# A four-layer diffusion trunk on one core: boundary operations moved into PSUM, and the first loads rearranged

## The chip, the cores and the metric

The kernel runs on one core of one Trainium2 chip. The metric is the device time of one execution in microseconds, lower being better; a kernel's time is the median of its runs. Only that time counts: neither the host nor the loading of the program is in it.

## What is computed

256 context tokens and 256 latent tokens of width 1024 go through four layers, and the latent ones come out. A layer is a token mixer and a SwiGLU feed-forward block (FFN, hidden width 2816). The mixers are differential attention (layers 0 and 3), windowed grouped-query attention (layer 1) and a bidirectional Mamba-2 scan (layer 2). In layer 3 only the latent tokens are carried past the mixer's keys and values. Each block sits in the same frame, where the six modulation vectors m of a layer come from a small product of the conditioning vector with `ada_w` (adaLN):

```python
m_lat = (act_lat @ ada_w[i] + ada_b[i]).reshape(b, N_MOD, 1, D)
u_lat = modulate(rmsnorm(h_lat, norm_g[i, 0]), m_lat[:, 0], m_lat[:, 1])   # t * (1 + scale) + shift
o_ctx, o_lat = mixer(u_ctx, u_lat, ...)
h_lat = h_lat + m_lat[:, 2] * rmsnorm(o_lat, norm_g[i, 1])
u_lat = modulate(rmsnorm(h_lat, norm_g[i, 2]), m_lat[:, 3], m_lat[:, 4])
h_lat = h_lat + m_lat[:, 5] * rmsnorm(swiglu(u_lat, ffn_w_in[i], ffn_w_out[i]), norm_g[i, 3])
```

The context tokens go through the same lines with `m_ctx`.

## The kernel before

**Products.** Everything is float32 made of two parts. A weight block of 128 x 1024 (512 KB) is loaded by a DMA that SP issues, ACT casts it to the high part `wh` (L261), and POOL, or for some blocks DVE, subtracts to get the low part `wl` (L263). Activations are split in the same way into `uh` and `ul`. A product is then three matmuls per 128 rows of weight: wh with uh, wh with ul, wl with uh (L285 to L287, L295 to L297).

**Tokens.** There are four tiles of 128 tokens: t0 and t1 are the context, t2 and t3 the latent ones. The residual stream `h` (`hall`) lies in SBUF, 128 tokens x 1024 a tile.

**A boundary** is what lies between the last product of a block and the first of the next, and it is done tile by tile. `project` (L495) multiplies out two halves of 512 columns into PSUM buffers "mm". Where partial sums exist it adds them into the SBUF tile `om` (L511). `gated` (L425) takes ACT's sum of squares of a half (L429), and DVE multiplies the half by the gate row into `om` (L430). `residual` (L432) adds the two sums (L436), makes a reciprocal root out of nine small 128x1 operations on DVE (`rsqrt`, L376 to L384) and adds the scaled 128x1024 tile to `h` in one instruction (L439). `normed` (L441) squares the new `h` on ACT (L447), makes a second root (L448, L376 to L384), scales the halves (ACT L456, DVE L454) into `sq`, and TensorE transposes them into PSUM "sm" (L460). `modulate` (L464) applies scale and shift, alternately on ACT (L475) and DVE (L473), into the SBUF tile `tm`, then casts `uh` (L477) and subtracts for `ul` (L478). The next block's matmuls read these.

**The FFN** (`unit` in L551) multiplies a gate into "mm" and an up part into "sc"; ACT takes Silu (L560), DVE multiplies into the SBUF tile `hd` (L561), ACT casts it (L563) and DVE subtracts (L564). There are 100 such units.

**adaLN.** The modulation weights come in blocks of 512 KB through a ring of four buffers "wa" (L308), 16 blocks for a pair of vectors. `ada_mm` multiplies four column groups into PSUM "ad" (L319); after the sixteenth ACT copies it out (L325), TensorE transposes it (L334), and `ada_finish` adds the bias (L341), adds 1 to a scale (L345) and multiplies by the norm's gain (L346).

**The start** (`run`, L1353): the context tiles are normed and copied to `oall` (L1370), the first 16 adaLN blocks run through the ring, three weight blocks are loaded, the latent half of `h` is loaded once the third is there (L1376, L1377), and the context tiles are modulated. The layer-0 mixer needs SBUF that `h` occupies, so `h_spill` (L703) writes it to DRAM (L708) and `h_reload` brings it back.

**Order.** A scheduler places the instructions of each engine once, when the program is built; each engine's queue is then worked off strictly in order. PSUM has eight buffers of 512 columns: three "mm", two "sc", two "sm", one "ad".

Of the kernel before, what the change touches and what calls it, by code (L numbers as in the profile page):

```python
# [177 lines left out]
class Trunk:  # L178
# [246 lines left out]
    def gated(self, src, t, x, row, ss):  # L425

        nc = self.nc
        q = self.t([P, 512], "tm", 2)
        nc.scalar.activation(q, src, AF.Square, scale=1.0 / 32, accum_out=ss[:, x : x + 1])  # L429
        nc.vector.tensor_tensor(out=self.om[t][:, 512 * x : 512 * x + 512], in0=src, in1=row, op=AL.mult)  # L430

    def residual(self, t, ss):  # L432

        nc = self.nc
        y, m = (self.t([P, 1], f"rs_{x}1", 4) for x in ("y", "m"))
        nc.vector.tensor_scalar(out=m, in0=ss[:, 0:1], scalar1=ss[:, 1:2], scalar2=EPS, op0=AL.add, op1=AL.add)  # L436
        self.rsqrt(y, m, 1)
        h = self.hall[:, t, :]
# [999 lines left out]
```

## Time and profile before

| | us |
|---|---|
| median of 3 runs | 2905.99 (2902.37 to 2906.01) |
| profiled execution | 2899.41 |
| its span | 2897.6, 37494 instructions |
| mean granted TensorE clock | 0.961 |

The profile is of one execution, and its times are microseconds from the start of the span. A busy share is a mean over the whole span. A timeline row says when an instruction started and how long it took, and in brackets how long its engine had been idle before it and what it waited for. The rows of a window give the busy time of each engine in one stretch; the stretch less TensorE's busy time (PE) is its idle time there.

### The profile page before, as it was taken

What the parts mean: (1) busy time and instruction counts of PE and PEld (TensorE: products, weight loads), DVE (VectorE), ACT (ScalarE), POOL (GpSimd) and SP (SyncE); (2) the same over time, 40 slices, a digit from 0 to 9 for tenths busy, and PEclk for the clock granted to TensorE, in tenths of its full rate; (3) what the DMA queues carried; (4) which work ended last, traced back from release to release, by engine and by line L of the source; (5) the groups of instructions that cost most, each with busy time, mean ns of one, the idle gap of its engine ahead of it and who ended that gap; (6) DMA issues with size and microseconds to landing.
All of it is one profiled execution on the core that took longest, in us unless ns stands there. A gap on an engine that the chain in (4) does not pass through costs nothing. (4 is left out here: it accounts for less than half of the span.)

```text
span 2897.6 us, 37494 instructions
## 1 busy us (share of the span) xinstructions
PE 2620.8 (90%) x14134; PEld 2110.0 (73%) x14134; DVE 1574.4 (54%) x2955; ACT 1236.4 (43%) x2439; POOL 1098.3 (38%) x525
## 2 busy tenths in 40 slices
PE   6999989999889989999888888879899998897898
PEld 3777677777776787777686666667777776786797
DVE  4676652222577662222588898866522226667444
ACT  4555443222357643222345555554432224554543
POOL 2322044334321053333333444433343343334585
PEclk8999999999999999999998999999999999999899
DMA  7433335544221145544231111132344442323352
GB/s 290 138 109 121 131 128 184 173 173 150 88 94 45 44 138 175 175 174 149 82 97 37 59 44 62 63 105 96 121 176 175 174 145 86 101 86 126 124 182 88
DMA packets 108325, 355.40 MB, mean 123 GB/s; under 512 B 14064, under 2 KB 24688, under 8 KB 105840
## 3 DMA queue, kind: packets, MB, share of 16 engines
q1 hardware_dynamic: 107568, 351.66, 36.0%
q8 instruction: 111, 1.82, 0.3%
q10 hardware_dynamic: 576, 1.34, 0.1%
q14 instruction: 70, 0.57, 0.1%
HBM read 329.36 MB, written 13.63 MB: 118 GB/s over the span
## 5 line engine op out<-in xcount | busy, mean ns | idle before, releaser
L263 POOL TENSOR_TENSOR wl<-wr,wh 128x1024 fp32r<-128x1024 f32 x356 | 863.5, 2432 | 1499.3 <-ACT wh L261 1360.0
L261 ACT ACTIVATE wh<-wr 128x1024 fp32r<-128x1024 f32 x356 | 376.0, 1057 | 809.4 <-PE mm L286 291.8
L285 PE MATMUL mm<-uh,wh 128*128 128x512 f32 (+1 forms) x1496 | 529.9, 355 | 16.3 <-ACT uh L477 15.0
L286 PE MATMUL mm<-ul,wh 128*128 128x512 f32 (+1 forms) x1496 | 526.9, 352 | 0.1
L287 PE MATMUL mm<-uh,wl 128*128 128x512 f32 (+1 forms) x1496 | 526.7, 352 | 0.0
L561 DVE TENSOR_TENSOR hd<-sc,sg 128x512 f32<-128x512 f32 (+1 forms) x100 | 56.9, 568 | 603.6 <-PE sc L287 599.0
L285 PEld LDWEIGHTS mm<-uh,wh 128*128 128x128 f32 x1496 | 289.3, 194 | 73.7 <-ACT uh L477 15.9
L287 PEld LDWEIGHTS mm<-uh,wl 128*128 128x128 f32 x1496 | 289.4, 193 | 34.4 <-issue 3.6
L286 PEld LDWEIGHTS mm<-ul,wh 128*128 128x128 f32 x1496 | 289.8, 194 | 32.5 <-issue 1.5
L285 PE MATMUL sc<-uh,wh 128*128 128x512 f32 (+1 forms) x800 | 273.7, 342 | 0.0
L287 PE MATMUL sc<-uh,wl 128*128 128x512 f32 (+1 forms) x800 | 273.7, 342 | 0.0
L286 PE MATMUL sc<-ul,wh 128*128 128x512 f32 (+1 forms) x800 | 273.6, 342 | 0.0
L296 PE MATMUL mm<-wh,hid 128*128 128x512 f32 x616 | 244.6, 397 | 0.0
L297 PE MATMUL mm<-wl,hid 128*128 128x512 f32 x616 | 244.0, 396 | 0.0
L295 PE MATMUL mm<-wh,hid 128*128 128x512 f32 x616 | 243.6, 396 | 0.0
L564 DVE TENSOR_TENSOR hid<-hd,hid 128x512 fp32r<-128x512 f32 (+1 forms) x100 | 207.5, 2075 | 65.8 <-ACT hid L563 65.8
L285 PEld LDWEIGHTS sc<-uh,wh 128*128 128x128 f32 x800 | 153.1, 191 | 17.6 <-issue 0.8
L286 PEld LDWEIGHTS sc<-ul,wh 128*128 128x128 f32 x800 | 153.2, 191 | 16.9
L287 PEld LDWEIGHTS sc<-uh,wl 128*128 128x128 f32 x800 | 153.2, 192 | 16.8
L595 DVE TENSOR_TENSOR o<-mm,o 128x512 f32<-128x512 f32 x84 | 58.0, 691 | 157.8 <-PE mm L297 157.8
L295 PEld LDWEIGHTS mm<-wh,hid 128*128 128x128 f32 x616 | 115.7, 188 | 35.9 <-ACT hid L563 4.2
L263 POOL TENSOR_TENSOR wl<-wa,wh 128x1024 fp32r<-128x1024 f32 x49 | 118.9, 2426 | 59.2 <-ACT wh L261 58.8
(300 smaller groups left out, 4851.5 us busy)
## 6 DMA issues: line engine op xcount, KB each, us to landing
wa<-in_adaw SPq DMA_DIRECT2D x192, 512.0 KB, 5.2
wr<-in_fin SPq DMA_DIRECT2D x154, 512.0 KB, 3.5
wr<-in_fout SPq DMA_DIRECT2D x77, 512.0 KB, 3.5
wr<-in_ssi SPq DMA_DIRECT2D x40, 512.0 KB, 3.5
wr<-in_daqk SPq DMA_DIRECT2D x24, 512.0 KB, 3.8
wa<-in_fin SPq DMA_DIRECT2D x22, 512.0 KB, 3.6
hspill<-h SPq DMA_DIRECT2D x8, 1024.0 KB, 4.0
h<-hspill SPq DMA_DIRECT2D x8, 1024.0 KB, 6.3
```

Source lines behind the costliest of these rows:

```text
L261: nc.scalar.activation(h, raw, AF.Copy)
L263: eng.tensor_tensor(out=l, in0=raw, in1=f32(h), op=AL.subtract)
L285: mm(out, wh, ah[ka][:, a:b], start=j == 0, stop=False)
L286: mm(out, wh, al[ka][:, a:b], start=False, stop=False)
L287: mm(out, wl, ah[ka][:, a:b], start=False, stop=j == len(todo) - 1)
L295: mm(out, ah[ka][:, tk], wt.h[:, kw, :], start=j == 0, stop=False)
L296: mm(out, al[ka][:, tk], wt.h[:, kw, :], start=False, stop=False)
L297: mm(out, ah[ka][:, tk], wt.l[:, kw, :], start=False, stop=j == len(todo) - 1)
L561: nc.vector.tensor_tensor(out=hd[:, :w], in0=pu[:, :w], in1=sg[:, :w], op=AL.mult)
L564: nc.vector.tensor_tensor(out=hl[:, a:b], in0=hd[:, :w], in1=f32(hh[:, a:b]), op=AL.subtract)
L595: nc.vector.tensor_tensor(out=o, in0=ps, in1=o, op=AL.add)
```

## The change

The two halves of a projection stay in the PSUM buffer that they were multiplied into: half 0 in "mm", half 1 in "sc". The partial sum is added and the gate row multiplied in place. The residual is two instructions of 512 columns, half 0 to `h`, half 1 to its PSUM buffer, which the squares and the scaling read directly; ACT copies it to `h` after the transposes (`settle`). The reciprocal root has six 128x1 operations instead of nine, all of the form tensor times per-partition scalar, with the squares scaled by G to fit. `modulate` works in place in PSUM, the FFN unit multiplies in place in its "sc" buffer, and `ada_finish` works in PSUM with the 1 added to the bias once at setup. At the start the first 12 adaLN blocks get buffers of their own (pool "first"), the other 4 the ring's; the context norm stays in PSUM ("sm" for t0, "sc" for t1); the latent half of `h` is loaded behind the first two weight blocks. The first `h_spill` writes nothing, since `h` is still the input `h0`.

```diff
@@ ada_load, ada_finish
-        raw = self.t([P, 2, 512], "wa", self.ADA_T)
+        raw = self.t([P, 2, 512], "wa", self.ADA_T) if pool is None else self.t([P, 2, 512], "w0", 12, pool=pool)
...
-            tt(out=mv, in0=pj[:, :, :, 0:2], in1=bias.unsqueeze(3).to_broadcast([P, 2, 4, 2]), op=AL.add)
+            tt(out=mv if n is None else pj, in0=pj, in1=bias.to_broadcast([P, 2, 4, 2]), op=AL.add)
             if n is not None:
-                if j in (1, 4):
-                    nc.vector.tensor_scalar(out=m, in0=m, scalar1=1.0, scalar2=None, op0=AL.add)
-                tt(out=m, in0=m, in1=self.ng[:, i, n, :].unsqueeze(2).to_broadcast([P, KD, 2]), op=AL.mult)
+                gain = self.ng[:, i, n, :].rearrange("p (q f) -> p q f", q=2).unsqueeze(3).to_broadcast([P, 2, 4, 2])
+                tt(out=mv, in0=pj, in1=gain, op=AL.mult)
@@ new: rsqrt1, squares, root, settle
+        ts(out=b.bitcast(I32), in0=m.bitcast(I32), scalar1=-0.5, scalar2=1597463007.0 - 2.0**31, op0=AL.mult, op1=AL.add)
+        ts(out=a, in0=b, scalar1=b, scalar2=m, op0=AL.mult, op1=AL.mult)
+        ts(out=a, in0=a, scalar1=-10.0 / 3, scalar2=a, op0=AL.add, op1=AL.mult)
+        ts(out=b, in0=a, scalar1=5.0, scalar2=b, op0=AL.add, op1=AL.mult)
+        ts(out=a, in0=b, scalar1=b, scalar2=m, op0=AL.mult, op1=AL.mult)
+        ts(out=y, in0=a, scalar1=-64.0 / 3, scalar2=b, op0=AL.add, op1=AL.mult)
...
+        self.nc.scalar.activation(q, src, AF.Square, scale=G / 32, accum_out=ss)
...
+        self.nc.scalar.activation(self.hall[:, t, 512:], hp, AF.Copy)
@@ residual
-        nc.vector.scalar_tensor_tensor(out=h, in0=self.om[t], scalar=y, in1=h, op0=AL.mult, op1=AL.add)
+        for x in range(2):
+            h = self.hall[:, t, 512 * x : 512 * x + 512]
+            self.nc.vector.scalar_tensor_tensor(
+                out=pss[1] if x else h, in0=pss[x], scalar=y, in1=h, op0=AL.mult, op1=AL.add
+            )
@@ normed, modulate
-        nc.scalar.activation(n, h, AF.Square, scale=1.0 / 32, accum_out=ss)
+        for x in range(2):
+            self.squares(hs[x], ss[:, x : x + 1])
...
+        if hp is not None:
+            self.settle(t, hp)
...
-                nc.vector.tensor_scalar(out=tm[:, k], in0=src[:, k], scalar1=a, scalar2=b, op0=AL.mult, op1=AL.add)
+                nc.vector.tensor_scalar(out=src[:, k], in0=src[:, k], scalar1=a, scalar2=b, op0=AL.mult, op1=AL.add)
...
-        nc.vector.tensor_tensor(out=ul, in0=tm, in1=f32(uh), op=AL.subtract)
+        nc.vector.tensor_tensor(out=ul, in0=src, in1=f32(uh), op=AL.subtract)
@@ project
-                ps = self.psum("mm")
+                ps = pss[t, x] = self.psum("sc" if x else "mm")
...
-                    nc.vector.tensor_tensor(out=src, in0=ps, in1=src, op=AL.add)
-                self.gated(src, t, x, rows[s, x], ss[t])
+                    nc.vector.tensor_tensor(out=ps, in0=ps, in1=o, op=AL.add)
+                self.squares(ps, ss[t][:, x : x + 1])
+                nc.vector.tensor_tensor(out=ps, in0=ps, in1=rows[s, x], op=AL.mult)
@@ ffn unit
-                nc.vector.tensor_tensor(out=hd[:, :w], in0=pu[:, :w], in1=sg[:, :w], op=AL.mult)
+                nc.vector.tensor_tensor(out=pu[:, :w], in0=pu[:, :w], in1=sg[:, :w], op=AL.mult)
...
-            nc.vector.tensor_tensor(out=hl[:, a:b], in0=hd[:, :w], in1=f32(hh[:, a:b]), op=AL.subtract)
+            nc.vector.tensor_tensor(out=hl[:, a:b], in0=pu[:, :w], in1=f32(hh[:, a:b]), op=AL.subtract)
@@ h_spill
+            self.hs = self.ins["h0"]
+            return self.t([P, KD * NT], "h")
@@ run
-                early[t, g] = self.oall[:, 4 * g : 4 * g + 4, t * P : (t + 1) * P]
-                self.nc.scalar.activation(early[t, g], ps, AF.Copy)
-        self.ada_flush(first, 1)
...
+            for t in range(16):
+                self.ada_load(*self.adaq.pop(0), None if t >= 12 else pool)
+            for n in range(2):
+                self.load_w(n)
+            self.nc.sync.dma_start(out=self.hall[:, 2:4], in_=self.ins["h0"][:, 2:4])
+            for t in TILES["c"]:
+                for g, ps in enumerate(self.normed(t, tag=("sm", "sc")[t])):
+                    early[t, g] = ps
+            while self.adaw:
+                self.ada_mm()
+            self.ada_finish("mm")
```

In the lists of instructions that follow, a name ends in the number of its buffer, and `out<-in` stands with the shape that is written.

The boundary of layer 3 between mixer and FFN, DVE, tile t2, before: gate multiply (L430), first root (L436 to L384) and residual (L439).

```order
L430 TENSOR_TENSOR o_84<-mm_22008,dq_21900 128x512
L436 TENSOR_SCALAR rs_m_4008_22037<-ss_21950 128x1
L376 TENSOR_SCALAR rs_y_4007_22036<-rs_m_4008_22037 128x1
L377 TENSOR_SCALAR rs_h_4009_22039<-rs_m_4008_22037 128x1
L378 TENSOR_TENSOR rs_a_4010_22040<-rs_y_4007_22036 128x1
L379 TENSOR_TENSOR rs_a_4010_22040<-rs_a_4010_22040,rs_m_4008_22037 128x1
L380 SCALAR_TENSOR_TENSOR rs_a_4010_22040<-rs_a_4010_22040 128x1
L381 SCALAR_TENSOR_TENSOR rs_y_4007_22036<-rs_a_4010_22040,rs_y_4007_22036 128x1
L382 TENSOR_TENSOR rs_a_4010_22040<-rs_y_4007_22036 128x1
L383 TENSOR_TENSOR rs_a_4010_22040<-rs_a_4010_22040,rs_h_4009_22039 128x1
L384 SCALAR_TENSOR_TENSOR rs_y_4007_22036<-rs_a_4010_22040,rs_y_4007_22036 128x1
L439 SCALAR_TENSOR_TENSOR h_21885<-o_84,rs_y_4007_22036,h_21885 128x1024
```

The same piece with the change:

```order
L532 TENSOR_TENSOR sc_21841<-sc_21841,dq_21733 128x512
L442 TENSOR_SCALAR rs_m_3929_21869<-ss_21783 128x1
L387 TENSOR_SCALAR rs_b_3931_21872<-rs_m_3929_21869 128x1
L388 TENSOR_SCALAR rs_a_3932_21873<-rs_b_3931_21872,rs_m_3929_21869 128x1
L389 TENSOR_SCALAR rs_a_3932_21873<-rs_a_3932_21873 128x1
L390 TENSOR_SCALAR rs_b_3931_21872<-rs_a_3932_21873,rs_b_3931_21872 128x1
L391 TENSOR_SCALAR rs_a_3932_21873<-rs_b_3931_21872,rs_m_3929_21869 128x1
L392 TENSOR_SCALAR rs_y_3930_21871<-rs_a_3932_21873,rs_b_3931_21872 128x1
L452 SCALAR_TENSOR_TENSOR h_21718<-mm_21785,rs_y_3930_21871,h_21718 128x512
L452 SCALAR_TENSOR_TENSOR sc_21841<-sc_21841,rs_y_3930_21871,h_21718 128x512
L442 TENSOR_SCALAR rs_m_3936_21887<-rs_s_3933_21882 128x1
```

The gate multiply and the residual now name PSUM buffers (`mm`, `sc`) where `o` stood, the root is seven instructions instead of ten, and every 128x1 one is a TENSOR_SCALAR.

The boundary between layer 0's FFN and layer 1's mixer, PE, the transposes of t2 (L460) among the mixer's first context matmuls, before:

```order
L285 MATMUL mm_6800<-uh_82,wh_6226 128x256
L286 MATMUL mm_6800<-ul_83,wh_6226 128x256
L287 MATMUL mm_6800<-uh_82,wl_6227 128x256
L285 MATMUL mm_6800<-uh_82,wh_6226 128x256
L460 MATMUL sm_6558<-cst_base_67,sq_6543 128x128 x4
L460 MATMUL sm_6564<-cst_base_67,sq_6543 128x128 x4
L286 MATMUL mm_6800<-ul_83,wh_6226 128x256
L287 MATMUL mm_6800<-uh_82,wl_6227 128x256
```

The same with the change (the transposes are L479):

```order
L284 MATMUL mm_6706<-uh_84,wh_6168 128x256
L285 MATMUL mm_6706<-ul_85,wh_6168 128x256
L286 MATMUL mm_6706<-uh_84,wl_6169 128x256
L284 MATMUL mm_6706<-uh_84,wh_6168 128x256
L479 MATMUL sm_6498<-cst_base_67,sq_6496 128x128 x4
L479 MATMUL sm_6504<-cst_base_67,sq_6496 128x128 x4
L285 MATMUL mm_6706<-ul_85,wh_6168 128x256
L286 MATMUL mm_6706<-uh_84,wl_6169 128x256
```

Before, 40 matmuls of the mixer stand between the FFN's last matmul and these transposes; with the change 10 do.

The start, SP, from the last two of the first 16 adaLN loads on, before:

```order
L308 DMA wa_198<-in_adaw 128x1024
L308 DMA wa_202<-in_adaw 128x1024
L260 DMA wr_229<-in_daqk 128x1024
L260 DMA wr_235<-in_daqk 128x1024
L260 DMA wr_271<-in_daqk 128x1024
L1344 DMA cst_att_378<-in_cst_att 128x640
L260 DMA wr_277<-in_dav 128x1024
L1377 DMA h_72<-in_h 128x2048
L260 DMA wr_283<-in_dav 128x1024
L770 DMA sublnr_391<-in_subln 128x1
L708 DMA hspill<-h_72 128x2048 x2
```

With the change, from the thirteenth of them on:

```order
L307 DMA wa_114<-in_adaw 128x1024
L307 DMA wa_116<-in_adaw 128x1024
L307 DMA wa_118<-in_adaw 128x1024
L307 DMA wa_120<-in_adaw 128x1024
L259 DMA wr_122<-in_daqk 128x1024
L259 DMA wr_128<-in_daqk 128x1024
L1399 DMA h_72<-in_h 128x2048
L259 DMA wr_261<-in_daqk 128x1024
L259 DMA wr_267<-in_daqk 128x1024
L259 DMA wr_273<-in_dav 128x1024
L1370 DMA cst_att_370<-in_cst_att 128x640
```

The load of the late half of `h` (`h_72<-in_h`) stands behind five weight blocks before (one of them ahead of this piece) and behind two with the change, and the two `hspill` writes are gone.

## Rows read from the trace of the kernel before

**Rows 1.** The page, part 1: busy time of each engine.

```profile
PE 2620.8 (90%) x14134; PEld 2110.0 (73%) x14134; DVE 1574.4 (54%) x2955; ACT 1236.4 (43%) x2439; POOL 1098.3 (38%) x525
```

**Rows 2.** Windows, seven boundaries: stretch, length, busy by engine, PEclk, DMA share, GB/s.

```profile
372.00:388.00 16.00, 8.27 (x46) 5.84 (x45) 12.05 (x19) 6.31 (x9) 9.63 (x5) 0.81 0.83 292
767.00:812.00 45.00, 31.23 (x179) 27.37 (x178) 36.40 (x79) 23.37 (x43) 22.39 (x12) 0.85 0.40 132
1012.00:1042.00 30.00, 21.63 (x124) 17.89 (x122) 22.78 (x38) 17.31 (x32) 20.31 (x8) 0.89 0.60 210
1415.00:1456.00 41.00, 28.48 (x157) 25.00 (x156) 31.70 (x68) 20.02 (x37) 19.31 (x12) 0.83 0.40 129
2004.00:2048.00 44.00, 30.80 (x167) 25.71 (x167) 33.59 (x75) 21.50 (x36) 20.11 (x8) 0.81 0.43 144
2424.00:2476.00 52.00, 34.55 (x191) 30.70 (x190) 38.07 (x84) 25.37 (x47) 22.93 (x12) 0.80 0.40 128
2663.00:2702.00 39.00, 16.58 (x80) 13.63 (x80) 25.95 (x60) 18.34 (x33) 11.76 (x5) 0.69 0.22 67
```

**Rows 3.** Windows, four short stretches (columns as in rows 2).

```profile
0.00:5.00 5.00, 0.00 (x0) 0.00 (x0) 0.27 (x1) 1.50 (x2) 2.29 (x8) 1.00 0.63 203
10.00:15.00 5.00, 5.00 (x22) 1.75 (x18) 2.39 (x15) 2.21 (x4) 0.00 (x0) 1.00 1.03 411
392.00:395.00 3.00, 3.00 (x28) 3.00 (x27) 2.72 (x12) 1.67 (x2) 0.00 (x0) 1.00 0.02 8
2041.00:2044.00 3.00, 3.00 (x16) 3.00 (x16) 2.27 (x6) 2.46 (x6) 0.00 (x0) 0.50 0.11 45
```

**Rows 4.** Timeline, 2669 to 2684 us: start, us, instruction, idle before and releaser.

```profile
2669.08 2.35 DVE L381 SCALAR_TENSOR_TENSOR rs_y<-rs_a,rs_y 128x1 f32<-128x1 f32 x1
...
2671.38 2.35 POOL L263 TENSOR_TENSOR wl<-wa,wh 128x1024 fp32r<-128x1024 f32 x1
...
2671.47 2.27 DVE L382 TENSOR_TENSOR rs_a<-rs_y 128x1 f32<-128x1 f32 x1
...
2673.77 2.26 DVE L383 TENSOR_TENSOR rs_a<-rs_a,rs_h 128x1 f32<-128x1 f32 x1
...
2683.16 0.66 PE L460 MATMUL sm<-cst_base,sq 128*128 128x128 f32 x2 [11.07 <-DVE sq L454]
```

**Rows 5.** Instructions by line, DVE: count, ns min/median/max, first to last, forms.

```profile
L430 DVE TENSOR_TENSOR o<-o,grow x28: 680/692/2901, 742.5 to 2890.2; 128x512 f32<-128x512 f32 x28
...
L430 DVE TENSOR_TENSOR o<-mm,dq x12: 675/690/692, 337.1 to 2688.7; 128x512 f32<-128x512 f32 x12
...
L448 DVE TENSOR_SCALAR rs_m<-rs_s x30: 144/154/156, 8.8 to 2693.6; 128x1 f32<-128x1 f32 x30
...
L473 DVE TENSOR_SCALAR tm<-sm,m,m x108: 396/410/413, 56.5 to 2698.8; 128x128 f32<-128x128 f32 x108
...
L473 DVE TENSOR_SCALAR tm<-o,m,m x8: 339/343/2375, 37.1 to 47.4; 128x128 f32<-128x128 f32 x8
...
L454 DVE TENSOR_SCALAR sq<-h,rs_y x30: 485/486/2645, 10.6 to 2695.3; 128x512 f32<-128x512 f32 x30
```

**Rows 6.** Timeline, 2404 to 2416 us, a boundary chain with no weight subtraction beside it.

```profile
2404.56 0.69 DVE L511 TENSOR_TENSOR o<-mm,o 128x512 f32<-128x512 f32 x1 [3.43 <-PE mm L297]
...
2413.57 1.09 PE L460 MATMUL sm<-cst_base,sq 128*128 128x128 f32 x8 [0.41 <-ACT sq L456]
```

**Rows 7.** Timeline, the start of the program.

```profile
32.81 0.60 ACT L325 ACTIVATE sq<-ad 128x512 f32<-128x512 f32 x1 [15.65 <-PE ad L319]
...
41.93 4.55 DVE L473 TENSOR_SCALAR tm<-o,m,m 128x128 f32<-128x128 f32 x2
...
47.26 1.01 PE L285 MATMUL mm<-uh,wh 128*128 128x256 f32 x3 [12.95 <-ACT uh L477]
```

**Rows 8.** The page, part 5: costliest groups (busy us, mean ns of one, idle before).

```profile
L261 ACT ACTIVATE wh<-wr 128x1024 fp32r<-128x1024 f32 x356 | 376.0, 1057 | 809.4 <-PE mm L286 291.8
...
L564 DVE TENSOR_TENSOR hid<-hd,hid 128x512 fp32r<-128x512 f32 (+1 forms) x100 | 207.5, 2075 | 65.8 <-ACT hid L563 65.8
```

More of the change, by code (lines that the diff above doesn't have):

```diff
@@ L23 @@
 NTT = NT // P
+G = 1024.0 / 27
 DEPTH = 4
@@ L423, in gate_rows, with squares, root, residual @@
         return rows
-    def gated(self, src, t, x, row, ss):
-        nc = self.nc
[L428 to L438, printed above, removed]
-        nc.vector.scalar_tensor_tensor(out=h, in0=self.om[t], scalar=y, in1=h, op0=AL.mult, op1=AL.add)
-    def normed(self, t):
-        nc = self.nc
-        y, m, ss = (self.t([P, 1], f"rs_{x}1", 4) for x in ("y", "m", "s"))
-        n = self.t([P, D], "sq", 2)
-        h = self.hall[:, t, :]
-        nc.scalar.activation(n, h, AF.Square, scale=1.0 / 32, accum_out=ss)
-        nc.vector.tensor_scalar(out=m, in0=ss, scalar1=EPS, scalar2=None, op0=AL.add)
-        self.rsqrt(y, m, 1)
-        out = []
+    def squares(self, src, ss):
+        q = self.t([P, 512], "tm", 2)
+        self.nc.scalar.activation(q, src, AF.Square, scale=G / 32, accum_out=ss)
+    def root(self, ss):
+        m = self.t([P, 1], "rs_m1", 4)
+        self.nc.vector.tensor_scalar(
+            out=m, in0=ss[:, 0:1], scalar1=ss[:, 1:2], scalar2=EPS * G * G, op0=AL.add, op1=AL.add
+        )
+        return self.rsqrt1(m)
+    def residual(self, t, ss, pss):
+        y = self.root(ss)
+        for x in range(2):
+            h = self.hall[:, t, 512 * x : 512 * x + 512]
+            self.nc.vector.scalar_tensor_tensor(
+                out=pss[1] if x else h, in0=pss[x], scalar=y, in1=h, op0=AL.mult, op1=AL.add
+            )
+    def settle(self, t, hp):
+        self.nc.scalar.activation(self.hall[:, t, 512:], hp, AF.Copy)
+    def normed(self, t, hp=None, tag="sm"):
+        nc = self.nc
+        hs = [self.hall[:, t, :512], self.hall[:, t, 512:] if hp is None else hp]
+        ss = self.t([P, 2], "rs_s1", 4)
+        for x in range(2):
+            self.squares(hs[x], ss[:, x : x + 1])
+        out = []
+        y = self.root(ss)
+        n = self.t([P, D], "sq", 2)
         for g in range(2):
@@ L1340, in setup @@
         nc.scalar.dma_start(out=self.ng, in_=ins["ng"])
+        for j in (1, 4):
+            b = self.adab[:, :, 8 * j : 8 * j + 8]
+            nc.vector.tensor_scalar(out=b, in0=b, scalar1=1.0, scalar2=None, op0=AL.add)
     def consts(self, name, pool):
@@ L1366, in run @@
         early = {}
[L1367 to L1387 removed]
+        with self.tc.tile_pool(name="first", bufs=1) as pool:
+            for t in range(16):
[9 more added lines that the diff above has]
+            self.ada_finish("mm")
+        for t in TILES["c"]:
+            for g in range(2):
+                self.modulate(early[t, g], m[0], m[1], t, g)
+        for n in range(2, 6):
+            self.load_w(n)
+        for t in TILES["l"]:
+            self.prenorm(m[0], m[1], t)
         for n, (i, mix, ff) in enumerate(self.layers):
@@ L1393, in run, with after @@
                 with self.tc.tile_pool(name=f"mix{i}", bufs=1) as pool:
-                    def after(t):
+                    def after(t, hp):
                         self.ada_flush(i, 4)
-                        self.prenorm(m[3], m[4], t)
+                        self.prenorm(m[3], m[4], t, hp)
                     for c in (("att",), ("att", "band"), ("ssd",))[i % 3]:
```

71 lines of the change are left out of this document (28 added, 43 removed).

## The prediction

> **What bounds the kernel now.** I began with the busy times on the page [rows 1]: TensorE (PE) is at work for 90% of the span and no other engine for more than 54%. A change that leaves the matmuls alone can only win where TensorE stands still, so I went to the windows next and looked for the idle time. Seven stretches hold most of what matters here [rows 2]: in each, one block's last product gives way to the next block's first. Stretch less busy PE gives 7.73, 13.77, 8.37, 12.52, 13.20, 17.45 and 22.42 us, 95.5 us in all. Inside an FFN there is nothing to win: 28 matmuls fill three microseconds out of three [rows 3].
>
> Then the timeline shows what a boundary waits for [rows 4]. Three operations on 128x1 numbers, which the same engine does in a sixth of a microsecond elsewhere, take 2.35, 2.27 and 2.26 us; each runs beside a weight subtraction on POOL, of which one stands there with 2.35 us. TensorE waits 11.07 us for what hangs on them. Last, I asked by line which forms are hit [rows 5]. The gate multiply takes up to 2901 ns where both tensors lie in SBUF (`o`, `grow`), never over 692 where one lies in PSUM (`mm`). The modulation out of PSUM has a maximum of 413 ns in 108, the same out of SBUF reaches 2375, and a 128x512 scaling out of SBUF 2645. The 128x1 TENSOR_SCALAR at L448 stays at 156 in 30. So the stall belongs to operations whose tensors all lie in SBUF while POOL works, small TENSOR_SCALARs excepted.
>
> **The change, part by part.**
>
> *Boundary operations.* With the change each large one has an operand in PSUM, and each 128x1 one is a TENSOR_SCALAR; by the rows above none of them stalls. What is left is the chain without stalls. It is seen at one place without POOL beside it: 9.0 us from the add at 2404.56 to the transposes at 2413.57 [rows 6]. Each of the two roots in it loses three of ten operations of about 0.15 us [rows 5], -0.9 in all. The scaling from PSUM is at most a 690 ns operation where it was 486 [rows 5], +0.2. So the chain becomes 8.3 us. The copy `settle` comes behind the transposes and holds an "sc" buffer some 0.6 us longer, the 128x512 copy of [rows 7]; ACT has the room for 28 of them.
>
> What covers this chain? At layer 0's FFN, t2's transposes come behind t3's 48 matmuls of 512 columns and 10 of 256. At 28 of 256 columns in 3 us [rows 3], 0.107 each and 0.214 for 512, that is 11.3 us against 8.3. t3's transposes have 98 matmuls of 256 columns ahead of them, 10.5 us, against 8.3 and what of t2's modulation (about 3) DVE and ACT put in between. So it fits, just. Weight casts of 1.06 us [rows 8] stand in ACT's queue between the links. I leave 3 us idle at each of the six boundaries that have context work to hide behind (bounds 1 and 6). At layer 3's mixer there is none: TensorE has nothing to do between the last projection and the first transposed tile, and I leave 12 (8.3 for one chain and nothing else, to 16 for one and a half with modulation). Left: 18 + 12 = 30 of 95.5, so **-65.5** (bounds -81.5 and -43.5).
>
> A rule speaks against the change. The one operation here that PSUM makes dearer is the scaling, 0.2 us in a chain that now loses up to 2.2 us per stall. The Trainium skill ("VectorE: DVE Perf Modes", Rules for kernel authors) says of elementwise work on matmul output to accept the lowest rate from PSUM, or to copy to SBUF first if many operations follow, and here some eight do; by that advice the old kernel is the right one, and the change would lose those 0.2 us for each of 28 tiles, at most 5.7 us. The rows decide otherwise, as the advice says nothing of POOL beside it.
>
> *The clock.* After such an idle part TensorE's granted clock is 0.50, the 1.2 GHz level, where it is 1.00 (2.4 GHz) inside the FFN: 16 matmuls in 3 us instead of 28 [rows 3], 1.3 us lost per 3 us. If half of the six boundaries no longer drop, **-4** (bounds 0, and -10 for all with a longer slow part).
>
> *The start.* Sixteen adaLN blocks are 8.39 MB, with the context half of `h` (1.05) and constants 9.7 MB. The first 5 us move 1.0 MB at 203 GB/s, the rest 8.7 MB at 411 [rows 3] takes 21.2 us: the last block lands at 26.2 instead of some 31.5, since the copy out of PSUM at 32.81 [rows 7] follows its products by little over a microsecond. The weight block that had been among them goes behind them, and no load waits for a ring buffer. That is 5.3 us. Behind it two modulations take 4.55 us where two of 0.34 would do [rows 5, 7], and the addition of 1 is gone from this path. The first main matmul, at 47.26 [rows 7], should start at about 38; its weights land by 29 and the late half of `h` by 31.5. Since the first matmuls then wait for one another's inputs, I take **-8.5** (bounds -5, the loads alone, and -10).
>
> *The FFN.* L564 takes 2075 ns in the mean [rows 8] and should fall to some 690 for 512 columns. DVE has the room, and TensorE was full, so 0. Holding the "sc" buffer through cast and subtraction, 1.3 us longer, is covered: the second buffer and the "mm" products give 72 matmuls, 7.7 us at 256 columns, until it is wanted. If that cover went, the third rival would hold.
>
> *The spill* of layer 0 removes two writes of 1 MB that no chain waited for: 0; it cannot cost. *The end*: the last tile has one copy of 0.6 more and a shorter root, **+0.4** (bounds 0 and 1).
>
> Sum: -65.5 - 4 - 8.5 + 0.4 = -77.6. The profiled execution took 2899.4, so 2821.8. The median of the runs stands 6.6 us above it; hence **2828**. With all bounds at their good end it is 2899.4 - 101.5 + 6.6 = 2804.5, at their poor end 2899.4 - 47.5 + 6.6 = 2858.5. A measurement can tell about 0.2%, 6 us.
>
> **The rivals.**
>
> *The next wait takes over.* Both roots freed, the chain still passes ACT some seven times per tile (two squares, two squares of the new `h`, a scaling, the casts), in order behind weight casts of 1.06 us [rows 8], and PSUM buffers come free later (two "sc" for halves, for t1's and t3's residual). With half a cast of wait per pass and two tiles, that is 7 us per boundary, and 14 at layer 3: 56 left, -39.5, and -5 at the start, none at the clock: 2861.5. For it: the chain fits only just. Against: in [rows 4] TensorE waits for DVE, not for ACT, and the sums of the windows leave ACT half idle. Chance 0.16.
>
> *The small operations stall too,* so that the change does not do what it says. The rebuilt roots read two per-partition scalars from SBUF besides their tensor, which L448 does not. If three stalls of about 2.15 us (2.3 less 0.15) [rows 4, 5] remain at each of seven boundaries, 45 us come back: 2873. The Trainium skill ("SBUF — State Buffer", Who interferes with whom) lets a tensor_scalar whose operands meet certain conditions take both of DVE's read ports, and then it shuts out POOL or waits for it; on 128x1 the trace disagrees, 156 at most, on 128x512 it agrees, 2645. Chance 0.05.
>
> *Slower: the FFN waits for its PSUM.* A unit's "sc" buffer is now free only after cast and subtraction, both in queues with weight work. TensorE then waits in each of 100 units [rows 8]. The gain of 77.6 us is used up at 0.78 us per unit; at 1.2 the time is 2828 + 120 = 2948. For it: two buffers only, which boundaries share. Against: the 7.7 us of cover above. Chance 0.03.
>
> *All gaps close.* If the six boundaries leave nothing, layer 3's leaves 8 and the clock stays up, -87.5 - 9.6 - 10 + 6.6 on 2899.4: 2799. Chance 0.06.
>
> **How the numbers follow.** The forecast has 0.70. Its own range, 2804.5 to 2858.5, and the first rival's 2861.5 with as much again above make 2805 to 2872, which leaves out the two slower rivals and most of the last, 0.14. Faster by over 0.2% in all cases but the third and a small rest: 0.95; within 0.2% 0.02; slower 0.03.
>
> **What would show it.** In the new profile the longest gate multiply, residual, scaling and modulation should stand within a few per cent of their medians, and the 128x1 operations at 0.14 to 0.21 us. PE's idle time should be about 3 us in six boundary windows and 12 in the seventh, the first main matmul at about 38 us, the FFN's subtraction at about 690 ns with TensorE full beside it. I am wrong if 128x1 operations of 2.3 us are still there (second rival), if PE's idle time at the boundaries stays above 50 us with ACT or a copy as the releaser (first), or if PE waits for "sc" inside an FFN (third).

## The result and the profile after

| | before | changed |
|---|---|---|
| median | 2904.65 us (2902.37 to 2906.01, 4 runs) | 2813.37 us (2808.11 to 2817.54, 4 runs) |
| profiled execution | 2899.41 | 2808.11 |
| span | 2897.6 | 2806.3 |
| granted TensorE clock | 0.961 | 0.975 |

The ratio is 0.9686, 95% interval 0.9666 to 0.9705: 91 us faster. The forecast was 2828, range 2805 to 2872. The changed kernel's profiled execution is the fastest of its four.

The busy times of the changed kernel, as in [rows 1]:

```profile
PE 2603.2 (93%) x14134; PEld 2098.6 (75%) x14134; DVE 1329.2 (47%) x2802; ACT 1239.4 (44%) x2523; POOL 1089.5 (39%) x525
```

TensorE's idle time (span less busy) falls from 276.8 to 203.1 us, and its busy time by 17.6 us with the same 14134 matmuls. Where this happened is seen best by counting matmuls, since both kernels have the same number of them. These are the windows of the changed kernel between the same matmuls, by number, as the seven of [rows 2], with the same columns:

```profile
354.13:363.14 9.01, 6.61 (x45) 4.16 (x44) 3.85 (x12) 7.29 (x13) 8.43 (x5) 1.00 0.75 231
741.08:774.21 33.13, 29.75 (x179) 26.59 (x177) 24.55 (x68) 23.36 (x48) 21.05 (x12) 0.95 0.53 178
973.37:996.35 22.98, 20.90 (x122) 15.74 (x121) 14.31 (x40) 18.08 (x34) 18.91 (x8) 0.93 0.63 203
1368.87:1397.89 29.02, 27.12 (x157) 24.06 (x156) 20.73 (x59) 21.29 (x43) 18.14 (x12) 0.94 0.62 189
1946.38:1979.46 33.08, 29.41 (x167) 25.16 (x166) 23.51 (x65) 22.91 (x44) 18.97 (x8) 0.90 0.50 144
2354.06:2393.26 39.20, 31.17 (x191) 28.50 (x190) 24.12 (x67) 25.17 (x52) 21.04 (x12) 0.87 0.53 180
2581.39:2609.91 28.52, 18.12 (x80) 15.45 (x79) 17.64 (x50) 19.04 (x39) 11.76 (x5) 0.71 0.32 93
```

Idle time is now 2.40, 3.38, 2.08, 1.90, 3.67, 8.03 and 10.40 us, 31.9 where it was 95.5; busy time in them falls from 171.5 to 163.1. The third column from the right, the granted clock (a mean over a window of parts at 1.00, which is 2.4 GHz, and at 0.50, which is 1.2 GHz), is 0.87 to 1.00 in the first six where it was 0.80 to 0.89.

The instructions by line, DVE, of the changed kernel (columns as in [rows 5]): gate multiply, scaling, modulation, the FFN's subtraction, and three operations of the root.

```profile
L532 DVE TENSOR_TENSOR mm<-mm,grow x14: 685/700/700, 717.1 to 2787.0; 128x512 f32<-128x512 f32 x14
...
L532 DVE TENSOR_TENSOR sc<-sc,grow x14: 698/700/700, 728.4 to 2798.3; 128x512 f32<-128x512 f32 x14
...
L473 DVE TENSOR_SCALAR sq<-sc,rs_y x25: 740/751/752, 332.6 to 2601.3; 128x512 f32<-128x512 f32 x25
...
L473 DVE TENSOR_SCALAR sq<-h,rs_y x4: 486/489/1902, 11.5 to 46.0; 128x512 f32<-128x512 f32 x4
...
L492 DVE TENSOR_SCALAR sm<-sm,m,m x112: 405/419/423, 30.7 to 2604.9; 128x128 f32<-128x128 f32 x112
...
L583 DVE TENSOR_TENSOR hid<-sc,hid x100: 414/691/693, 369.0 to 2775.7; 128x512 fp32r<-128x512 f32 x54, 128x256 fp32r<-128x256 f32 x46
...
L387 DVE TENSOR_SCALAR rs_b<-rs_m x58: 135/153/155, 10.0 to 2799.1; 128x1 int32<-128x1 int32 x58
...
L388 DVE TENSOR_SCALAR rs_a<-rs_b,rs_m x58: 264/272/275, 10.2 to 2799.3; 128x1 f32<-128x1 f32 x58
...
L392 DVE TENSOR_SCALAR rs_y<-rs_a,rs_b x58: 203/214/219, 11.3 to 2800.4; 128x1 f32<-128x1 f32 x58
```

Every maximum here stands within 4% of its median but one (L583 has two shapes, and its maximum is that of the larger): the scaling of a tile that still lies in SBUF (`sq<-h`, used where a tile comes from the input) reaches 1902. L583, the old L564 [rows 8], is down from 2075 to 569 ns in the mean.

The start in the changed kernel's timeline, to set beside [rows 7]:

```profile
28.26 0.60 ACT L324 ACTIVATE sq<-ad 128x512 f32<-128x512 f32 x1 [14.25 <-PE ad L318]
...
36.47 0.79 PE L284 MATMUL mm<-uh,wh 128*128 128x256 f32 x2 [6.90 <-ACT uh L496]
```

By stage, from the start times of the same matmul numbers in both traces (length in us, TensorE's idle time in brackets). The start is the first 1000 matmuls. The boundary stretches are cut much wider than the windows above, 699.6 us before where the windows have 267, and take in parts of the mixer and the FFN on either side. One execution each; the experiments below are in it too.

```
                 start          mixers          7 boundaries    FFN
before           214.7 (40.2)   904.2 (115.2)   699.6 (112.3)   1069.7 (0.0)
changed          200.4 (30.0)   896.7 (113.5)   629.4 (50.1)    1069.5 (0.0)
e1 pool_writes   193.2 (23.5)   809.0 (43.1)    612.6 (41.2)    1069.7 (0.0)
e2 root_nine     205.3 (34.8)   897.5 (114.4)   693.6 (104.4)   1069.8 (0.0)
e3 root_pad      201.7 (30.4)   901.8 (111.0)   631.5 (53.1)    1069.7 (0.0)
e4 resid_sbuf    202.4 (31.6)   899.5 (109.8)   637.3 (61.4)    1069.7 (0.0)
e5 start_new     208.9 (39.2)   906.4 (116.4)   702.2 (111.0)   1069.7 (0.0)
e6 start_old     208.2 (35.0)   901.4 (111.6)   632.1 (50.4)    1080.2 (0.0)
e7 start_ring    204.1 (33.0)   900.6 (110.5)   632.7 (52.1)    1069.7 (0.0)
e8 ffn_sbuf      201.3 (31.9)   900.8 (112.8)   634.9 (52.5)    1069.7 (0.0)
e9 split_before  204.6 (34.1)   867.9 (89.6)    674.9 (92.3)    1071.9 (1.7)
e10 split_after  195.7 (26.1)   863.2 (89.0)    627.0 (51.5)    1069.7 (0.0)
e11 mod_sbuf     206.3 (33.8)   903.5 (114.0)   662.1 (75.8)    1070.1 (0.0)
e12 split_mix    199.6 (27.4)   863.1 (80.1)    638.6 (60.8)    1069.7 (0.0)
```

From before to changed the boundaries gain 70.2 us, the start 14.3, the mixers 7.5 and the FFN 0.2. Idle time accounts for 62.3, 10.2 and 1.7 of the first three. Most of the mixers' gain is in layer 2's: 492.5 us before, 486 in this execution and 487 in e2's, but 490 to 492 in six other variants that changed nothing in it either. So some 4 of the 7.5 come and go from one variant to the next, and why is not shown.

### The profile page after: what moved, and what is told of

Same layout as the page of the kernel before. It is cut to its first block, busy times and chain, and to the rows that moved or that the text cites. A ratio compares the mean times of both kernels' runs of the same rounds, so it can differ in the third digit from the quotient of the medians.

```text
span 2806.3 us, 37430 instructions
## 1 busy us (share of the span) xinstructions
PE 2603.2 (93%) x14134; PEld 2098.6 (75%) x14134; DVE 1329.2 (47%) x2802; ACT 1239.4 (44%) x2523; POOL 1089.5 (39%) x525
## 5 line engine op out<-in xcount | busy, mean ns | idle before, releaser
L580 DVE TENSOR_TENSOR sc<-sc,sg 128x512 f32<-128x512 f32 (+1 forms) x100 | 57.6, 576 | 754.8 <-PE sc L286 745.2
L294 PE MATMUL mm<-wh,hid 128*128 128x512 f32 x504 | 200.6, 398 | 0.0
L296 PE MATMUL mm<-wl,hid 128*128 128x512 f32 x504 | 200.0, 397 | 0.0
L295 PE MATMUL mm<-wh,hid 128*128 128x512 f32 x504 | 199.6, 396 | 0.0
L1183 POOL TENSOR_TENSOR cd<-h,dtt 128x512 f32<-128x512 f32 x64 | 78.7, 1235 | 121.4 <-DVE dm L1193 114.5
L294 PEld LDWEIGHTS mm<-wh,hid 128*128 128x128 f32 x504 | 94.7, 188 | 30.0 <-issue 4.2
```

The costliest lines, as they stand in the source:

```text
L294: mm(out, ah[ka][:, tk], wt.h[:, kw, :], start=j == 0, stop=False)
L295: mm(out, al[ka][:, tk], wt.h[:, kw, :], start=False, stop=False)
L296: mm(out, ah[ka][:, tk], wt.l[:, kw, :], start=False, stop=j == len(todo) - 1)
L580: nc.vector.tensor_tensor(out=pu[:, :w], in0=pu[:, :w], in1=sg[:, :w], op=AL.mult)
L1183: getattr(nc, self.ENG_CD).tensor_tensor(out=cd.rearrange("p (c l) -> p c l", c=4), in0=cbm[d].rearrange("p (c l) -> p c l", c=4), in1=sel ...
```

## The experiments

**Theory A** is the prediction's: DVE operations whose tensors all lie in SBUF wait for POOL's weight subtraction, and the gain is those waits. **Theory B**, the rival: the gain comes from a shorter chain and less work on DVE, whatever POOL does. The kernel before ran beside each variant on the same chip, at 2903 to 2904 us, and the ratios are to that; medians are of four runs (ten for e5). Differences to the changed kernel are between medians from different chips, on which the kernel before stands within 2 us.

### e1: the old kernel with a POOL that only writes

```diff
-        eng.tensor_tensor(out=l, in0=raw, in1=f32(h), op=AL.subtract)
+        for _ in range(2):
+            eng.memset(f32(l), 0.0)
```

> The kernel before, with one edit: instead of subtracting (reading two tiles in SBUF), POOL writes zeros into the low weight part, twice over, so the low part of every weight is missing from the result. Theory A (DVE operations with all tensors in SBUF wait while POOL reads SBUF): the longest gate multiply out of SBUF falls from 2901 ns to about 700 and the 128x1 tensor_tensor operations from 2342 to about 160; TensorE's idle time in the seven boundaries falls from about 95 us to 30 to 45; the time is 2830 to 2850. Theory B (the gain comes from shorter chains and less DVE work, whatever POOL does): nothing of that changes and the time stays at 2900 to 2908.

2693.02 us (2691.09 to 2695.71), ratio 0.9277 (0.9262 to 0.9293). By line, DVE: gate multiply, a root operation, and the scaling out of SBUF.

```profile
L431 DVE TENSOR_TENSOR o<-o,grow x28: 684/693/694, 697.1 to 2686.4; 128x512 f32<-128x512 f32 x28
...
L383 DVE TENSOR_TENSOR rs_a<-rs_y x74: 150/159/166, 10.4 to 2688.3; 128x1 f32<-128x1 f32 x58, 128x4 f32<-128x4 f32 x16
...
L455 DVE TENSOR_SCALAR sq<-h,rs_y x30: 483/487/2412, 11.0 to 2491.0; 128x512 f32<-128x512 f32 x30
```

The gate multiply and the roots don't stall any more, though POOL still writes to SBUF 810 times. The scaling does: it has one tensor, in SBUF, and takes up to 2412 ns beside POOL's writes alone. In this trace operations with two tensors in SBUF stall only beside the tensor_tensor operations that POOL has left in layer 2's mixer. So reading is what holds the first kind, and writing still holds the scaling. The old chains, ten-operation roots, SBUF tiles and all, then leave 41 us of idle time at the boundaries, less than the change does. Theory B falls. The time is far below what was expected, since the mixers lose 95 us too: their DVE work has its tensors in SBUF as well. This bounds what POOL's reading costs and does not price it: a POOL that waits for no load and no cast also has its part ready earlier, and its single instructions are shorter (955 ns in the median). The shortness by itself does not explain the roots, which stall beside pieces of 0.75 us in e9.

### e2 and e3: the old root back, and a root as long without its forms

```diff
@@ e2
-G = 1024.0 / 27
+G = 1.0
-        return self.rsqrt1(m)
+        y = self.t([P, 1], "rs_y1", 4)
+        self.rsqrt(y, m, 1)
+        return y
@@ e3, in rsqrt1
+        for _ in range(3):
+            ts(out=a, in0=a, scalar1=1.0, scalar2=None, op0=AL.mult)
```

> The changed kernel with the old nine-operation root (tensor_tensor and scalar_tensor_tensor on 128x1) put back, all else as changed. Theory A: these operations stall again beside POOL, up to 2.3 us each, 15 to 40 us in all: 2828 to 2853. Theory B: three more operations of about 0.16 us in each of two roots a tile, 1 us a boundary: 2816 to 2822, no operation over 0.3 us.

> The changed kernel with three more 128x1 tensor_scalar operations in each root, a multiplication by 1, so that a root is as long as the old one by count but has none of its forms. Theory A: only the added length, some 0.5 us a root: 2814 to 2822, no operation over 0.3 us. Theory B: as much as the old root gives in the run beside it, to within 3 us.

e2: 2877.17 (2876.0 to 2880.28), ratio 0.9913 (0.9898 to 0.9928). e3: 2815.75 (2812.74 to 2818.55), ratio 0.9699 (0.9683 to 0.9715), which overlaps the changed kernel's. The same count of operations costs 64 us in the one form and some 2 in the other. The timeline of e2 at layer 3's boundary shows why. Below it stands one line of e2's roots over the whole run (busy us, mean ns), then the operation that e3 adds:

```profile
2657.30 2.35 POOL L262 TENSOR_TENSOR wl<-wr,wh 128x1024 fp32r<-128x1024 f32 x1 [3.30 <-DMA wa<-in_fout]
...
2658.26 1.40 DVE L375 TENSOR_TENSOR rs_a<-rs_y 128x1 f32<-128x1 f32 x1
...
2659.60 2.35 POOL L262 TENSOR_TENSOR wl<-wa,wh 128x1024 fp32r<-128x1024 f32 x1
...
2659.70 2.26 DVE L376 TENSOR_TENSOR rs_a<-rs_a,rs_m 128x1 f32<-128x1 f32 x1
```

```profile
L376 DVE TENSOR_TENSOR rs_a<-rs_a,rs_m 128x1 f32<-128x1 f32 x58 | 30.4, 524 | 1.5
```

```profile
L393 DVE TENSOR_SCALAR rs_a<-rs_a x174: 134/153/157, 11.1 to 2809.2; 128x1 f32<-128x1 f32 x174
```

Each stalled operation ends where POOL's ends. e2's roots have seven such lines with 58 operations each; their means are 206 to 524 ns instead of some 160, which makes 95 us of stalls, and the time is 64 us longer. So 70% of the gain is lost when the old root alone goes back in. That is not the root's share of the gain: in the kernel before the roots stall for some 48 us only (their lines are summed below, at e9), the parts taken back one by one (e2, e4, e6, e8, e11) come to 134 us where the whole gain is 91, and the new root in the old kernel was not run. Theory A had 15 to 40: the sign was right, the size was not.

### e4 and e11: gate and residual, and modulation, back in SBUF

```diff
@@ e4, project and residual
-                ps = pss[t, x] = self.psum("sc" if x else "mm")
+                ps = pss[t, x] = self.psum("mm")
...
+                o = self.om[t][:, 512 * x : 512 * x + 512]
+                nc.vector.tensor_tensor(out=o, in0=src, in1=rows[s, x], op=AL.mult)
...
+        self.nc.vector.scalar_tensor_tensor(out=h, in0=self.om[t], scalar=y, in1=h, op0=AL.mult, op1=AL.add)
@@ e11, modulate
+        tm = self.t([P, 4, P], "tm", 2)
...
-        nc.vector.tensor_tensor(out=ul, in0=src, in1=f32(uh), op=AL.subtract)
+        nc.vector.tensor_tensor(out=ul, in0=tm, in1=f32(uh), op=AL.subtract)
```

> The changed kernel with the added partial sum, the gate multiply and the residual put back into the SBUF tile (one 128x1024 residual, both halves in mm buffers, no copy back to h); root, modulation, FFN and start stay as changed. Theory A: gate multiplies where a partial sum was added and the residual reach 2.8 to 3.3 us again in some of the tiles, 10 to 30 us: 2823 to 2843. Theory B: the shorter roots are most of the gain: 2811 to 2818.

> The changed kernel with the modulation written to an SBUF tile again; it still reads PSUM, the cast reads the tile, and the subtraction for ul has both inputs in SBUF. Stall theory: some of 60 subtractions take up to 2.9 us, those of the last tile of a boundary on the path: plus 3 to 12 us, 2816 to 2825. If the modulation's place does not count: 2811 to 2816.

e4: 2821.93 (2819.97 to 2823.99), ratio 0.9723 (0.9706 to 0.9741), 8.6 us above the changed kernel, just under the expected 10 to 30 and above what Theory B had; the gate multiply reaches 2867 ns again. e11: 2850.63 (2842.7 to 2853.89), ratio 0.9815 (0.9794 to 0.9835): 37 us, where 3 to 12 were expected. The stall itself is the expected one. What was missed is who else uses the tile, as e11's timeline shows at the first boundary:

```profile
354.97 2.47 DVE L498 TENSOR_TENSOR ul<-tm,uh 128x512 fp32r<-128x512 f32 x1 [1.13 <-ACT uh L497]
...
357.47 0.60 ACT L437 ACTIVATE tm<-mm 128x512 f32<-128x512 f32 x1 [1.24 <-DVE ul L498]
...
374.97 1.97 PE L479 MATMUL sm<-cst_base,sq 128*128 128x128 f32 x8 [7.38 <-ACT sq L475]
```

`tm` has two buffers, and the squares of a projection's half write into the same ones. The subtraction stalls for 2.47 us, it holds `tm`, and the square of the next tile's half on ACT waits for it (`<-DVE ul L498`), and that tile's chain follows the square. Over the run the stalls of this subtraction make some 19 us (60 times 1003 ns in the mean, less 692), and ACT waits 11.1 us for `tm` behind it, in 20 places. How much of the 37 each causes is not settled. Modulating in PSUM gives `tm` to the squares alone; the prediction counted this part of the change as stalls only.

### e5 to e7: the start

```diff
@@ e5: the kernel before with ada_load, ada_finish, setup, h_spill and run's start of the change
@@ e6: the changed kernel with run's start of the kernel before
@@ e7
             for t in range(16):
-                self.ada_load(*self.adaq.pop(0), None if t >= 12 else pool)
+                if t >= 4:
+                    self.ada_mm()
+                self.ada_load(*self.adaq.pop(0))
```

> The kernel before with the new start alone (12 buffers more for the first adaLN blocks, context norm kept in PSUM, late half of h behind two weight blocks, bias with 1 added once, adaLN finish in PSUM, no write of the first residual); boundaries, root and FFN as before. The table by matmul number gave 14.3 us to the first 1000 matmuls of the change, where the prediction had 8.5. If the start alone is worth that: 2888 to 2893, first main matmul at 36 to 38 us. If part of the 14.3 came from the boundary operations in it (norm and modulation of the latent tiles out of PSUM, shorter roots): 2893 to 2898.

> The changed kernel with the old start (ring of four for the first adaLN blocks, context norm copied to SBUF, late half of h behind three weight blocks); the boundaries and the first residual's write left out stay as changed. If start and boundaries simply add: 2813 plus 12 to 15, 2825 to 2829. If the boundary forms carry part of the start: 2819 to 2824.

> The changed kernel with its first 16 adaLN blocks through the ring of four, a product before each load after the fourth, all else as changed. If loads ahead of need are what the start gains: the last adaLN product is at about 31 us and the first main matmul at 40 to 43, 2817 to 2821. If the ring never held a load up (products follow the blocks closely, the order of the weights behind them is what counts): first main matmul at 36 to 38, 2811 to 2816.

e5: 2896.62 (2893.01 to 2900.39), ratio 0.9981 (0.9972 to 0.9991). The start alone is worth 6 us, and its trace says what holds it up:

```profile
28.53 0.60 ACT L325 ACTIVATE sq<-ad 128x512 f32<-128x512 f32 x1 [14.93 <-PE ad L319]
...
37.58 2.30 DVE L380 TENSOR_TENSOR rs_a<-rs_y 128x1 f32<-128x1 f32 x1
...
39.91 2.26 DVE L381 TENSOR_TENSOR rs_a<-rs_a,rs_h 128x1 f32<-128x1 f32 x1
...
42.29 0.72 DVE L471 TENSOR_SCALAR tm<-sc,m,m 128x128 f32<-128x128 f32 x2
...
43.41 1.01 PE L285 MATMUL mm<-uh,wh 128*128 128x256 f32 x3 [13.57 <-DVE sq L452]
```

The adaLN product is ready as early as in the changed kernel, 28.5 us, but the first main matmul waits until 43.4: two stalled operations in the root of a latent tile, 2.30 and 2.26 us, stand in DVE's queue ahead of the last context modulation (L471). So more than half of the start's gain (8.5 of 14.3 us in the stage table) needs the boundary forms. e7: 2819.02 (2813.91 to 2823.53), ratio 0.9709 (0.969 to 0.9728), not told apart from the changed kernel by time; by the trace the product is ready at 32.9 and the first main matmul starts at 38.6 instead of 36.5, between what its two theories expected, and the first thousand matmuls take 3.7 us longer. e6: 2833.88 (2832.92 to 2837.13), ratio 0.9763 (0.9747 to 0.9779), 20.5 us above the changed kernel where at most 15 were expected. The stage table puts 7.8 of it in the start and 10.7 in the FFN stretches, where TensorE stands still in neither kernel and its matmuls follow each other at 0.231 us instead of 0.227 in the median of the first FFN, as of the next two. Why, these runs do not show; without it e6 would stand at 2823, where the theory was that the boundary forms carry part of the start.

### e8: the FFN's product in SBUF again

```diff
+            hd = self.t([P, NT], "hd", 2, pool=pool)
...
-            nc.vector.tensor_tensor(out=hl[:, a:b], in0=pu[:, :w], in1=f32(hh[:, a:b]), op=AL.subtract)
+            nc.vector.tensor_tensor(out=hl[:, a:b], in0=hd[:, :w], in1=f32(hh[:, a:b]), op=AL.subtract)
```

> The changed kernel with the FFN's product in an SBUF tile again, all else as changed. Theory A with the prediction's 0 for the FFN: the subtraction takes up to 2.4 us again in most of 100 units, and the time stays within 0.2%, 2808 to 2819. Rival: the longer hold or shorter stall in the FFN counts at its ends, where the boundary's chain waits behind the last subtractions in DVE's queue, 1 to 2 us at each of four: 2818 to 2824.

2816.8 (2812.51 to 2821.59), ratio 0.9701 (0.9679 to 0.9724), the same as the changed kernel within the interval. The subtraction is back at its stall:

```profile
L584 DVE TENSOR_TENSOR hid<-hd,hid x100: 415/2430/2471, 372.8 to 2785.9; 128x512 fp32r<-128x512 f32 x54, 128x256 fp32r<-128x256 f32 x46
```

The FFN stretches stay at 1069.7 us. A stall of 2 us in most of a hundred units costs nothing while TensorE has work. The rival, a cost at the FFN's ends, is not ruled out: e8's boundary stretches are 5.5 us longer than the changed kernel's, though those of e3, e6 and e7 are 2 to 3 longer too.

### e9, e10 and e12: shorter POOL instructions

```diff
-        eng.tensor_tensor(out=l, in0=raw, in1=f32(h), op=AL.subtract)
+        fl = lambda x: x.rearrange("p k n -> p (k n)")
+        for c in range(4):
+            r = slice(c * kc * w // 4, (c + 1) * kc * w // 4)
+            eng.tensor_tensor(out=fl(l)[:, r], in0=fl(raw)[:, r], in1=fl(f32(h))[:, r], op=AL.subtract)
@@ e12: for the mixers' weights 8 instead of 4
```

> The kernel before, with POOL's weight subtraction of 128x1024 cut into four of 128x256; nothing else is changed. If a stalled DVE operation waits for the end of the one POOL instruction it met, the longest 128x1 tensor_tensor falls from 2342 ns to about 0.16 + 0.6 = 0.8 us and the longest gate multiply from 2901 to about 1.4 us, the boundary idle of 95 us falls to 45 to 65, and the time to 2820 to 2870. If POOL keeps the port as long as it has such work in its queue, the pieces following each other closely hold DVE as long as one large one: 2.3 us stays, 2895 to 2915.

> The changed kernel with POOL's weight subtraction cut into four of 128x256. If a stall lasts to the end of one POOL instruction: what is left of stalls, in the mixers above all (the run whose POOL only writes was 51 us shorter than the changed kernel there in layer 2 and 13 to 16 in layers 0 and 1), shrinks to a third or so: 2740 to 2795. If POOL keeps the port: 2810 to 2825, the added instructions costing POOL some 0.1 us each.

> The changed kernel with POOL's subtraction cut into four for FFN weights and into eight (128x128) for those of the mixers. If stalls scale with the length of one POOL instruction: the mixers gain some 10 us on the run with four pieces everywhere, 2752 to 2762. If the added time on POOL (about 0.17 us a piece, 3.8 us a weight block) makes it late for TensorE: the mixers wait for low weight parts, 2768 to 2790.

e9, the old kernel with nothing but shorter pieces on POOL: 2831.67 (2828.8 to 2833.5), ratio 0.9753 (0.9737 to 0.9768). By line, DVE:

```profile
L433 DVE TENSOR_TENSOR o<-o,grow x28: 678/693/1230, 725.1 to 2821.2; 128x512 f32<-128x512 f32 x28
...
L385 DVE TENSOR_TENSOR rs_a<-rs_y x74: 152/160/668, 10.4 to 2823.0; 128x1 f32<-128x1 f32 x58, 128x4 f32<-128x4 f32 x16
```

In the roots a stall lasts to the end of the one POOL instruction: 668 ns on this line and 755 at most on a 128x1 one, where it was up to 2.3 us. The time came out in the expected range, but not in the expected place: the boundaries keep 92 of 112 us of idle time, and the mixers gain 36 us. In the roots the shorter stalls are more numerous: 128x1 operations lose 47 us in all, 48 before (busy time of the nine lines of 58 less 0.158 us each). A chain of tiny operations meets every piece; a large operation mostly meets one.

Not always, and here the other theory of the expectation was right too. In layer 3's FFN four subtractions (L567) took 9.1, 10.9, 12.7 and 14.1 us, while 13 to 20 pieces on POOL followed each other without a gap. The last of them:

```profile
2779.60 14.07 DVE L567 TENSOR_TENSOR hid<-hd,hid 128x256 fp32r<-128x256 f32 x1 [0.92 <-ACT hid L566]
...
2790.60 2.80 POOL L266 TENSOR_TENSOR wl<-wa,wh 128x256 fp32r<-128x256 f32 x4
2795.49 0.75 POOL L266 TENSOR_TENSOR wl<-wr,wh 128x256 fp32r<-128x256 f32 x1 [2.09 <-ACT wh L261]
```

It ended only once POOL paused. TensorE stood still for 1.5 us meanwhile, until the product behind it in DVE's queue (L564) had freed a "sc" buffer: in this one place what the third rival had feared. Why these four waited through every piece and the roots did not is not shown.

e10, the same on the changed kernel: 2766.97 (2766.74 to 2767.37), ratio 0.9531 (0.9514 to 0.9547). It beats both kernels, 46 us below the changed one, and again most of it is in the mixers (33.5), whose own operations the change left as they were, and some in the start (4.7). The two gains add in part: against the kernel before they are 72.5 us for e9 and 91.3 for the change, 163.8 in sum, and 137.2 together. In the mixers e9's gain stays; at the boundaries, where e9 had 24.7 in the stage table, 2.4 are left. e12: 2782.32 (2781.18 to 2786.42), ratio 0.9591 (0.9575 to 0.9607): eight pieces gain the mixers nothing more in time, and the boundaries lose 11.6 us. The time lies in the range of its second theory, but POOL's weight subtraction is not among the longest waits of TensorE, so that theory is not shown either; 3.7 us of the loss are a wait for a small DMA at the sixth boundary, described below.

## Why the prediction was right, and where its steps were not

**The boundaries** were forecast at -65.5 us and gave -63.6 in the windows, left over 31.9 for 30: 21.5 in the six that have cover, for 18, and 10.4 at layer 3's, for 12. The cause is the forecast one (e1, and e2 against e3). The Trainium skill ("SBUF — State Buffer", Who interferes with whom) says that a DVE instruction with two SBUF inputs contends with a GpSimd instruction that reads SBUF and not with one that only writes; e1 agrees: the gate multiply takes 694 ns at most beside a writing POOL, 2901 beside a reading one.

**A step inside it failed:** "Each of the two roots in it loses three of ten operations of about 0.15 us, -0.9 in all." The timelines of the old and of the changed kernel, from a root's first operation to the residual, both without a stall:

```profile
2406.71 0.21 DVE L436 TENSOR_SCALAR rs_m<-ss 128x1 f32<-128x1 f32 x1
...
2408.50 1.28 DVE L439 SCALAR_TENSOR_TENSOR h<-o,rs_y,h 128x1024 f32<-128x1024 f32 x1
```

```profile
2586.37 0.20 DVE L442 TENSOR_SCALAR rs_m<-ss 128x1 f32<-128x1 f32 x1
...
2588.16 0.75 DVE L452 SCALAR_TENSOR_TENSOR h<-mm,rs_y,h 128x512 f32<-128x512 f32 x1
```

Both take 1.79 us. The new root has three operations fewer, but those that read two per-partition scalars take 272 ns and those that read one 214, where the old ones took 160. The scaling out of PSUM takes 751 ns where the prediction had 690 at most. So the chain became no shorter in time. That changes the gain little: e3's three further operations a root cost some 2 us in the whole. What the new root is worth is that it doesn't stall.

**The leftover of the sixth boundary,** 8.0 us for a forecast 3, is a wait that I did not look for. The changed kernel's timeline at the tail of t3's second root there:

```profile
2377.28 0.27 DVE L391 TENSOR_SCALAR rs_a<-rs_b,rs_m 128x1 f32<-128x1 f32 x1
...
2378.47 0.39 SPq L782 DMA_DIRECT2D tm<-in_lam  x1
...
2382.30 0.29 DVE L785 TENSOR_TENSOR tm<-tm 128x128 f32<-128x128 f32 x1 [4.75 <-DMA tm<-in_lam]
...
2382.51 0.21 DVE L392 TENSOR_SCALAR rs_y<-rs_a,rs_b 128x1 f32<-128x1 f32 x1
...
2383.53 1.97 PE L479 MATMUL sm<-cst_base,sq 128*128 128x128 f32 x8 [4.91 <-ACT sq L475]
```

The root's last operation (L392) stands in DVE's queue behind a small product for layer 3's lambda (L785), which waits 4.75 us for its DMA, issued only at 2378.47; TensorE waits 4.91 for what follows. In the old kernel that product waited for 1.59 us and lay outside the chain. e10 has 7.49 us of it and e12 11.20. Loading that tile earlier, in a buffer of its own, was not tried.

**The clock** was mis-sized: -4 (bounds 0 and -10) against -8.5 of busy time in the boundary windows (-10.0 in the six, +1.5 at layer 3's), and -17.6 in the whole trace: 4.1 of it in the start, 5.8 in the mixers. I had half of the six boundaries stay up, at 1.3 us each, from a low stretch of 3 us; in five of them the mean granted clock is now 0.90 or above. The low stretches had also been longer than 3 us: a mean of 0.85 over 45 us [rows 2] is 13.5 us at 1.2 GHz.

**The start** was forecast at -8.5 up to the first main matmul, which now starts 10.8 us earlier (36.47 for 47.26; 38 had been forecast). The product is ready 4.55 us earlier, for a forecast 5.3. From there to the first main matmul it takes 8.2 us where it took 14.5. The prediction priced the two slow modulations there and named the addition of 1 without a price; the old timeline shows a stall at that addition (L345) and one more at a subtraction (L478):

```profile
34.64 2.16 DVE L345 TENSOR_SCALAR m<-m 128x16 f32<-128x16 f32 x1
...
39.48 2.42 DVE L478 TENSOR_TENSOR ul<-tm,uh 128x512 fp32r<-128x512 f32 x1 [0.36 <-ACT uh L477]
```

The first thousand matmuls gain 14.3 us. Of the 3.5 behind the first main matmul 2.6 are busy time, at a mean granted clock of 0.98 where it was 0.96; the sum had left that part out. It had the mixers at nothing as well, without a reason, and they gave 7.5, of which some 4 are open as said above.

**The FFN** was forecast at 0 and gives 0.2 us; e8 shows the stall back and its stretches unchanged. **The end** is 0.6 us longer, for +0.4. **The spill** at 0 was not tried by itself. Between the two profiled executions the whole came to -91.3 where the sum had -77.6. The boundary term held by its mechanism; the rest of the gap is the clock, the start and the mixers, all taken too small.

**The rivals.** The small operations don't stall: those of the root take 275 ns at most, at L388. TensorE doesn't wait for "sc" in any FFN. The next wait did not take over as a whole. What is left at the boundaries does have ACT's scaling as its releaser, by the changed kernel's list of waits (us in total, times, longest), the wait of the sixth boundary included. It is 29 us where the transposes had waited 90 (66 for ACT's scaling and 24 for DVE's):

```profile
PE sm L479 <- ACT sq L475: 24.6, 8, 5.4
...
PE ad L479 <- ACT sq L475: 4.3, 1, 4.3
```

## What to carry to other kernels

Look in the trace for one form whose maximum is many times its median, and ask what runs on the other engines then; chains of tiny operations are hit hardest, because each of them can meet the other engine's instruction anew. Two cures helped here, and their gains added in part (137 of 164 us). One is to keep an operand of the waiting side in PSUM or, in a 128x1 operation, in a per-partition scalar; a 128x512 scaling out of SBUF still stalled with its per-partition scalar (1902 ns). The other is to cut the other engine's instructions short. A stall of 2 us was worth money only where TensorE had nothing else to do, as the FFN shows.
